# First norm of a diffusion layer: the last token range's column sums, diagonals and spread placed between the middle range's apply steps

## The chip, the cores and the metric

The kernel runs on one core of a Trainium2 chip. The metric is the device time of one execution in microseconds. A run of a kernel is a program of five engines that work side by side and wait for each other by semaphores: PE (matmuls), DVE and ACT (elementwise work, DVE with two tensors), POOL (elementwise work on data outside the matmul accumulators), and SP, which issues DMAs.

## The reference

One layer of a diffusion transformer on 1024 tokens of 1024 channels. After the token mixers, the part that matters here is the first layer norm and the first product of the feed-forward part:

```python
x = _layer_norm(DEEPNORM_ALPHA * x + gate1 * y, ln1_g[l], ln1_b[l])

h = x * (1.0 + scale2) + shift2
y = _conv_ffn(h, w_up[l], conv_w[l], conv_b[l], w_down[l])
...
def _layer_norm(x, g, b):
    mu = jnp.mean(xf, axis=-1, keepdims=True)
    var = jnp.mean(jnp.square(xf - mu), axis=-1, keepdims=True)
    return ((xf - mu) * lax.rsqrt(var + LN_EPS) * g + b).astype(x.dtype)
...
def _conv_ffn(h, w_up, conv_w, conv_b, w_down):
    u = h @ w_up
    ...  # u: convolution over 3 neighbouring tokens, one filter per channel, plus conv_b
    gate, val = jnp.split(u, 2, axis=-1)
    return (jax.nn.silu(gate) * val) @ w_down
```

## The kernel before

Data lie with channels on the 128 partitions: a tensor of 1024 channels is eight blocks f = 0 to 7 (or k, where it is summed over), each with the tokens along its row. Products in float32 are made of three matmuls with split operands (`mm3`, L90 to L92): each operand is a high part and a low part, so `B3` stands for a pair, its high part written by ACT and its low part (value minus high part) by DVE or POOL.

The first norm works on three token ranges, `LN1_S`: 0 to 511, 512 to 767 (the middle range here) and 768 to 1023 (the last range). A token's mean is a sum over partitions, so it is taken by matmuls. `ln_steps` returns a list of eleven steps for a range:

- `stats`: matmuls with a column of ones sum `zs` (the values) and `zq` (their squares) over the channels, L1157 and L1158, into the tile `sta`; then small DVE steps make mean and variance (`mva`, `m2a`, `rsa`, L1159 to L1162), POOL takes the power -1/2 (L1164), and DVE multiplies (`mra`, L1165).
- `diags`: DVE writes two diagonal matrices, `dgra` and `dgma` (L1105).
- `cast`, called the spread here: matmuls with a matrix of ones spread the diagonals over all partitions, into `bca` (L1174); ACT copies the mean's half to `mba` (L1177).
- eight apply steps, in the order f = 0, 4, 1, 5, 2, 6, 3, 7: DVE multiplies (L1182), DVE (f even, L1184) or POOL (f odd, L1186) subtracts, then `emit1` stores the block to DRAM, lets ACT write the high part of `B` and a copy `v` (L1202), and lets DVE or POOL write the low part (L1208).

Each step has a delay beside it. The steps lie in a list, `pend`. Every `mm3` on PE calls `tick` with its columns over 0.8, and `tick` runs the first step of the list as soon as its delay has passed; `drain(n)` runs all but the last n at once. So the list sets where PE's norm matmuls stand between its product matmuls. PE's order is the order of the code; the order of DVE, ACT, POOL and SP is set by a scheduler when the program is built, from the same code, and a step that comes elsewhere in the code can reorder rows of other work there.

After the mixers' last product (`y`), PE makes the up product. Its tiles are `u0_0`, `u1_0`, `u0_1`, `u1_1`, `u0_2`, `u1_2`, each 128 channels by 1024 tokens in the matmul accumulators (`big`, three buffers). The first three tiles are made for the first range, then for the middle range, then for the last range, so that the norm of a range has the products of the range before it as cover. From `u1_1` on a tile is made for all tokens at once. A fourth tile gets the buffer of the first, once its convolution has read it: ACT's L1364 and two DVE steps, L1365 and L1367, into `c0_0`.

```python
def big(name):
    return ps3.tile([P, T], F32, tag="big", name=name, bufs=3)
```

`build(k)`, for k = 0 to 3, forms sums of operand blocks for later products: `t13_k` and `t24_k`, each a first half and a second half, on DVE and POOL; then ACT casts to `T13h_k` and `T24h_k`, and DVE writes the low parts `T13l_k` and `T24l_k` (all L1208). Those steps are put into `pend` after the three ranges, and are first used when the tiles after `u1_2` are made, from 978.8 us on.

## Time and profile before

| | |
|---|---|
| median of 3 runs | 1578.71 us (1578.34 to 1579.38) |
| profiled execution | 1578.46 us, span 1576.7 us |
| PE busy | 1538.4 us, 98% of the span |
| DVE, ACT, POOL busy | 76%, 52%, 47% |
| sums of the last range on PE | from 915.04 us |
| spread of the last range on PE | from 920.76 us |
| first apply of the last range on DVE | 922.23 us |
| `u1_1` begins on PE | 946.12 us |

Rows of a timeline give the start in us from the span's start, the duration, the engine, the line, the operation, the tile written and the tiles read (buffer numbers left out), the shapes, and in brackets how long the engine stood idle before and what released it. Groups of equal rows are merged with a count. A row of a table of stretches gives the stretch, its length, the busy time of PE, PE's weight loads, DVE, ACT and POOL, then PE's granted clock (1.00 is full), the share of the DMA engines and GB/s.

### The profile page before, as it was taken

What the parts mean: (1) busy time and instruction counts of PE and PEld (TensorE: products, weight loads), DVE (VectorE), ACT (ScalarE), POOL (GpSimd) and SP (SyncE); (2) the same over time, 40 slices, a digit from 0 to 9 for tenths busy, and PEclk for the clock granted to TensorE, in tenths of its full rate; (3) what the DMA queues carried; (4) which work ended last, traced back from release to release, by engine and by line L of the source; (5) the groups of instructions that cost most, each with busy time, mean ns of one, the idle gap of its engine ahead of it and who ended that gap; (6) DMA issues with size and microseconds to landing.
All of it is one profiled execution on the core that took longest, in us unless ns stands there. A gap on an engine that the chain in (4) does not pass through costs nothing.

```text
span 1576.7 us, 22297 instructions
## 1 busy us (share of the span) xinstructions
PE 1538.4 (98%) x7804; PEld 1283.1 (81%) x7804; DVE 1199.0 (76%) x1768; ACT 813.8 (52%) x1450; POOL 740.2 (47%) x728
## 2 busy tenths in 40 slices
PE   9999999999999999989999999999999999999997
PEld 7888888888877787777688988888888888888887
DVE  6677976548888677788674788788888887657884
ACT  5323123368887667688430564444444444435552
POOL 0355423526666556555342454566667774021121
PEclk9999999999999999999999999999999999999998
DMA  9776662322247555440550222323334446996821
GB/s 372 270 234 234 224 232 90 110 79 59 63 127 158 130 134 132 115 87 18 179 174 27 92 69 96 118 96 117 109 108 118 110 113 186 367 266 210 258 101 54
DMA packets 112528, 230.00 MB, mean 146 GB/s; under 512 B 12992, under 2 KB 27840, under 8 KB 112320
## 3 DMA queue, kind: packets, MB, share of 16 engines
q1 hardware_dynamic: 97184, 199.72, 38.1%
q0 software_dynamic: 10400, 20.19, 8.4%
q10 hardware_dynamic: 4832, 8.68, 1.5%
q8 instruction: 61, 1.00, 0.3%
q14 instruction: 51, 0.42, 0.1%
HBM read 177.35 MB, written 65.86 MB: 154 GB/s over the span
## 4 chain that ended last, share of the span: by engine, by line
PE 87%; DVE 5%; ACT 3%; issue 2%; POOL 1%; DMA 0%; SPq 0%; DVEq 0%; ACTq 0%; POOLq 0%
PE ptr L611 5%; PE p L90 4%; PE p L91 4%; PE p L92 4%; PE g L90 4%; PE g L92 4%; PE g L91 4%; PE b L92 3%; PE b L91 3%; PE b L90 3%; PE av L632 2%; PE s L494 2%; PE av L633 2%; PE d L92 2%; PE c L92 2%; PE a L92 2%
## 5 line engine op out<-in xcount | busy, mean ns | idle before, releaser
L621 DVE TENSOR_TENSOR ptl<-ptr,pth 128x512 fp32r<-128x512 f32 x188 | 124.5, 684 | 28.0 <-ACT pth L620 26.0
L611 PE MATMUL ptr<-ident,p 128*128 128x128 f32 x816 | 126.8, 278 | 10.5 <-DVE ptl L621 8.2
L620 ACT CAST pth<-ptr 128x512 fp32r<-128x512 f32 x188 | 106.6, 588 | 57.8 <-PE ptr L611 34.2
L87 DVE TENSOR_TENSOR ld<-rd,hd 128x1024 fp32r<-128x1024 f32 x77 | 95.0, 1249 | 49.2 <-ACT hd L82 45.4
L506 ACT ACTIVATE p<-p,nm 128x1024 f32<-128x1024 f32 (+2 forms) x128 | 125.3, 981 | 10.7 <-DVE p L539 10.0
L611 PEld LDWEIGHTS ptr<-ident,p 128*128 128x128 f32 x816 | 93.6, 140 | 40.9 <-DVE ptl L621 13.9
L82 ACT CAST hd<-rd 128x1024 fp32r<-128x1024 f32 x77 | 79.4, 1049 | 82.2 <-PE p L92 58.4
L632 PE MATMUL av<-pth,VT 128*128 128x512 f32 x236 | 104.5, 443 | 0.7 <-ACT avs L638 0.5
L90 PE MATMUL p<-hd 128*128 128x512 f32 x264 | 103.2, 391 | 0.0
L87 POOL TENSOR_TENSOR wlg<-wg,whg 128x512 fp32r<-128x512 f32 x32 | 45.7, 1438 | 122.4 <-ACT whg L82 122.4
L92 PE MATMUL p<-hd,ld 128*128 128x512 f32 x264 | 102.7, 389 | 0.0
L91 PE MATMUL p<-ld,hd 128*128 128x512 f32 x264 | 102.7, 389 | 0.0
L90 PE MATMUL g<-hh,whg 128*128 128x512 f32 x256 | 99.9, 390 | 0.0
L92 PE MATMUL g<-hh,wlg 128*128 128x512 f32 x256 | 99.7, 389 | 0.0
L91 PE MATMUL g<-hl,whg 128*128 128x512 f32 x256 | 99.6, 389 | 0.0
L633 PE MATMUL av<-ptl,VT 128*128 128x512 f32 x236 | 97.7, 414 | 2.0 <-POOL ptl L87 1.8
L539 DVE TENSOR_SCALAR_CACHE_REDUCE p<-s,cvt,nmc 128x1024 f32<-128x1024 f32 x64 | 84.4, 1339 | 12.1 <-PE s L495 11.8
L494 PE MATMUL s<-KL,q 128*128 128x512 f32 (+2 forms) x192 | 76.0, 396 | 2.7 <-ACT p_x L506 2.0
L783 ACT ACTIVATE sg<-g,bgc 128x512 f32<-128x512 f32 x32 | 22.0, 687 | 97.0 <-PE g L92 92.0
L84 POOL TENSOR_SCALAR pth<-prw 128x512 fp32r<-128x512 f32 x48 | 31.0, 646 | 87.2 <-ACT prw L617 62.2
L495 PE MATMUL s<-KL,q 128*128 128x512 f32 (+2 forms) x192 | 71.7, 373 | 0.0
L82 ACT CAST wA<-ru 128x512 fp32r<-128x512 f32 x57 | 35.5, 623 | 67.8 <-PE d L92 36.2
(433 smaller groups left out, 5015.2 us busy)
## 6 DMA issues: line engine op xcount, KB each, us to landing
wml<-in_wmodT_dram SPq DMA_DIRECT2D x48, 512.0 KB
ru<-in_w_up_dram SPq DMA_DIRECT2D x38, 512.0 KB
rd<-td SPq DMA_DIRECT2D x55, 256.0 KB
rd<-sd SPq DMA_DIRECT2D x44, 256.0 KB
rd<-in_w_dn_dram SPq DMA_DIRECT2D x33, 256.0 KB
wm<-in_wmodT_dram SPq DMA_DIRECT2D x16, 512.0 KB
wg<-in_w_g_dram SPq DMA_DIRECT2D x32, 256.0 KB
sgd<-sg ACTq DMA_DIRECT2D x32, 256.0 KB
```

The lines of the kernel that those rows point to most:

```text
L82: nc.scalar.copy(hi, src)
L87: lo_eng.tensor_tensor(out=lo, in0=src, in1=hi.bitcast(F32), op=ALU.subtract)
L90: nc.tensor.matmul(ps, a[0], b[0], start=start, stop=False, skip_group_check=resumed)
L91: nc.tensor.matmul(ps, a[0], b[1], start=False, stop=False, skip_group_check=resumed)
L92: nc.tensor.matmul(ps, a[1], b[0], start=False, stop=stop, skip_group_check=resumed)
L494: nc.tensor.matmul(o, self.q[0][:, hs], ks, start=True, stop=False)
L506: nc.scalar.activation(p, s, AF.Exp, bias=nm[:, h:h + 1], scale=scale, accum_out=sm[:, h:h + 1])
L611: nc.tensor.transpose(tr[:, h * P:(h + 1) * P], self.pslice(h, n), ident)
L620: nc.scalar.copy(hi, tr)
L621: nc.vector.tensor_tensor(out=lo, in0=tr, in1=hi.bitcast(F32), op=ALU.subtract)
L632: nc.tensor.matmul(self.av, v, hi, start=first, stop=False)
L633: nc.tensor.matmul(self.av, v, lo, start=False, stop=self.left == 0)
```

## The change

The last range's steps are no longer put behind the middle range's. When the list gets them it still holds nine steps of the middle range: its spread and its eight applies. The new code puts the sums of the last range behind the fourth apply, its diagonals behind the seventh, its spread behind the eighth, and its applies behind that, with new delays for the three. The numbers of steps that `drain` leaves in the list follow from this.

```diff
-            if f == 6:
+            if f == 6 and si == 1:
                 pend += ln1(si)
+            elif f == 6:
+                (_, st), (_, dg), (_, ca), *ap = ln1(si)
+                n = len(pend) - 4
+                pend[:] = pend[:n] + [(300.0, st)] + pend[n:-1] + [(300.0, dg), pend[-1], (1800.0, ca)] + ap
...
-        drain((len(LN1_S) - 1 - si) * (KT + 3))
+        drain((2 * KT + 6, KT + 1, 0)[si])
```

The diff adds four lines, so line numbers behind it are 4 higher in the new kernel: the old L1367 is its L1371.

On PE, at the up product over the first range (the number behind a tile's name tells which range, k or tile it is, `B7_0` is block 7 for tokens 0 to 511, and the last number is only the buffer's), the piece of the difference at the old place of the sums and the new place of the spread is this:

```order
 L92 MATMUL u1_0_9880<-B6_0_9598,lwu1_0_9728 128x512
-L1157 MATMUL sta2_9997<-onec_70,zs1_9084 128x1
-L1158 MATMUL sta2_9997<-onec_70,zq1_9085 128x1
-L1157 MATMUL sta2_9997<-onec_70,zs1_9084 128x1
-L1158 MATMUL sta2_9997<-onec_70,zq1_9085 128x1
 L90 MATMUL u1_0_9880<-B7_0_9672,hwu1_0_9727 128x512
 L91 MATMUL u1_0_9880<-B7_0_9672,hwu1_0_9727 128x512
 L92 MATMUL u1_0_9880<-B7_0_9672,lwu1_0_9728 128x512
+L1174 MATMUL bca2_10014<-dgra2_9991,onesf_71 128x256
+L1174 MATMUL bca2_10014<-dgma2_9993,onesf_71 128x256
 L90 MATMUL u0_1_9881<-B0_0_9465,hwu0_1_9869 128x512
```

The sums now stand seven k steps further up, ahead of the first matmul of `u1_0`; the spread came six k steps up, from behind k = 5 of `u0_1`.

On DVE, at the end of the middle range's applies (`z` is the value, `bca1` the middle range's spread), the rows before are these:

```order
L1184 TENSOR_TENSOR z2_1_9097<-z2_1_9097,bca1_9891 128x256
L1208 TENSOR_TENSOR B1_1_9922<-v1_9923,B1_1_9922 128x256
L1182 TENSOR_TENSOR z3_1_9109<-z3_1_9109,bca1_9891 128x256
L1208 TENSOR_TENSOR B5_1_9933<-v1_9923,B5_1_9933 128x256
L1182 TENSOR_TENSOR z3_1_9109<-z3_1_9109,bca1_9891 128x256
L1159 TENSOR_SCALAR mva2_9993<-sta2_9997 128x4
L1161 TENSOR_TENSOR m2a2_9994<-mva2_9993 128x2
L1162 SCALAR_TENSOR_TENSOR rsa2_9995<-mva2_9993,m2a2_9994 128x2
L1208 TENSOR_TENSOR B3_1_9967<-v3_9968,B3_1_9967 128x256
L1165 TENSOR_TENSOR mra2_9996<-mva2_9993,rsa2_9995 128x2
L1105 TENSOR_TENSOR dgra2_10019<-ident_58,rsa2_9995 128x256
L1105 TENSOR_TENSOR dgma2_10021<-ident_58,mra2_9996 128x256
```

And from the small step `rsa` on, now:

```order
L1162 SCALAR_TENSOR_TENSOR rsa2_9944<-mva2_9942,m2a2_9943 128x2
L1184 TENSOR_TENSOR z2_1_9097<-z2_1_9097,bca1_9891 128x256
L1208 TENSOR_TENSOR B1_1_9922<-v1_9923,B1_1_9922 128x256
L1165 TENSOR_TENSOR mra2_9945<-mva2_9942,rsa2_9944 128x2
L1182 TENSOR_TENSOR z3_1_9109<-z3_1_9109,bca1_9891 128x256
L1208 TENSOR_TENSOR B5_1_9933<-v1_9923,B5_1_9933 128x256
L1105 TENSOR_TENSOR dgra2_9991<-ident_58,rsa2_9944 128x256
L1105 TENSOR_TENSOR dgma2_9993<-ident_58,mra2_9945 128x256
L1182 TENSOR_TENSOR z3_1_9109<-z3_1_9109,bca1_9891 128x256
L1208 TENSOR_TENSOR B3_1_9982<-v3_9983,B3_1_9982 128x256
```

All six small steps of the last range now stand ahead of the middle range's last L1182. On POOL the power, L1164, likewise moved ahead of the subtracts of f = 3 and 7.

On DVE, where the first convolution is reached (`c0_0` reads the accumulator of `u0_0`, and `t13_2`, `t24_2` and so on are the sums of `build`), the rows before are these:

```order
L1208 TENSOR_TENSOR T13l_1_10373<-t13_1_10342,T13h_1_10372 128x1024
L1208 TENSOR_TENSOR t13_2_10412<-v2_9947,z2_0_9094 128x512
L1365 SCALAR_TENSOR_TENSOR c0_0_10235<-u0_0_9879,cvt_69,c0_0_10235 128x1023
L1208 TENSOR_TENSOR t24_2_10427<-v2_9947,t13_2_10412 128x512
L1367 SCALAR_TENSOR_TENSOR c0_0_10235<-u0_0_9879,cvt_69,c0_0_10235 128x1023
```

And now:

```order
L1208 TENSOR_TENSOR T13l_1_10373<-t13_1_10342,T13h_1_10372 128x1024
L1208 TENSOR_TENSOR t13_2_10412<-v2_9962,z2_0_9094 128x512
L1208 TENSOR_TENSOR t24_2_10427<-v2_9962,t13_2_10412 128x512
L1208 TENSOR_TENSOR t13_3_10478<-v3_9983,z3_0_9106 128x512
L1208 TENSOR_TENSOR t24_2_10427<-z2_0_9094,t24_2_10427 128x512
L1208 TENSOR_TENSOR T13l_2_10443<-t13_2_10412,T13h_2_10442 128x1024
L1208 TENSOR_TENSOR T24l_2_10456<-t24_2_10427,T24h_2_10455 128x1024
L1369 SCALAR_TENSOR_TENSOR c0_0_10235<-u0_0_9879,cvt_69,c0_0_10235 128x1023
L1208 TENSOR_TENSOR t24_3_10481<-v3_9983,t13_3_10478 128x512
L1371 SCALAR_TENSOR_TENSOR c0_0_10235<-u0_0_9879,cvt_69,c0_0_10235 128x1023
```

`t13_3`, the second `t24_2`, `T13l_2`, `T24l_2` and `t24_3` moved ahead of the second step of `c0_0`. On ACT, `T13h_2` and `T24h_2` moved ahead of `c0_0`'s first step. The order of SP is the same, and so is that of every engine from the tiles behind `u1_2` on.

## The prediction

> **What bounds the kernel now.** I read the page first, then PE's waits over the whole run, then the busy time by stretches, then the timelines of PE, DVE, POOL and ACT from 905 to 950 us, where the change acts.

> ```profile
> span 1576.7 us, 22297 instructions
> PE 1538.4 (98%) x7804; PEld 1283.1 (81%) x7804; DVE 1199.0 (76%) x1768; ACT 813.8 (52%) x1450; POOL 740.2 (47%) x728
> PE u L91 <- DVE B L1208: 2.9, 1, 2.9
> 932.85:935.90 3.05, 0.17 (x3) 0.01 (x1) 3.05 (x4) 3.05 (x5) 3.05 (x3) 0.89 0.13 43
> 935.90:942.10 6.20, 6.20 (x29) 6.20 (x30) 6.20 (x5) 4.66 (x5) 3.54 (x3) 0.50 0.00 0
> 946.10:978.80 32.70, 32.70 (x147) 27.07 (x146) 29.74 (x27) 13.75 (x17) 12.15 (x8) 1.00 0.33 113
> 978.80:1540.00 561.20, 561.20 (x2548) 467.19 (x2547) 450.39 (x429) 274.46 (x362) 269.97 (x164) 1.00 0.53 160
> ```

> PE is busy for 98% of the span, so a gain must come out of its gaps. The third line is its only long wait near the change (one, of 2.9 us, the longest single one of the run): the up product over the last token range wants the low half of `B3`, which DVE has not written. The stretches (length, then busy time of PE, PEld, DVE, ACT and POOL, then PE's granted clock) show that it costs twice: PE stands for 3 us, and for the next 6.2 us works at clock 0.50. From 946.1 to 1540 PE has no gap, so whatever PE's arrival at 946.1 gains or loses is carried to the end whole.

> The wait's exact price, from PE's timeline:

> ```profile
> 923.02 0.28 PE L90 MATMUL u<-B,hwu 128*128 128x256 f32 x1
> ...
> 932.73 0.28 PE L90 MATMUL u<-B,hwu 128*128 128x256 f32 x1
> 935.90 0.58 PE L91 MATMUL u<-B,hwu 128*128 128x256 f32 x1 [2.88 <-DVE B L1208]
> 936.28 0.42 PE L92 MATMUL u<-B,lwu 128*128 128x256 f32 x1
> ...
> 942.04 0.29 PE L92 MATMUL u<-B,lwu 128*128 128x256 f32 x1
> ...
> 946.12 0.40 PE L90 MATMUL u<-B,hwu 128*128 128x512 f32 x1
> ```

> The 81 matmuls from 923.02 to 932.73 come every 0.120 us, the 27 from 936.28 to 942.04 every 0.213. At full pace the one at 935.90 would have started at 932.85 (3.05 lost), and the 28 up to 942.04 lost 6.14 - 28 x 0.120 = 2.78. So 5.83 us are to be had, 0.37%, and PE would begin `u1_1` (the row at 946.12) at 940.29.

> **The change, part by part.** Nothing is added or removed: the same four sum matmuls, seven small DVE and POOL steps, two spread matmuls and one copy stand elsewhere. None of them issues a DMA, and SP's queue has the same order. First, how much earlier the last range's applies (L1182 on) start:

> ```profile
> 910.28 0.39 PE L90 MATMUL u<-B,hwu 128*128 128x512 f32 x1
> ...
> 914.82 0.39 PE L92 MATMUL u<-B,lwu 128*128 128x512 f32 x1
> 915.04 0.28 PE L1157 MATMUL sta<-onec,zs 128*128 128x1 f32 x2
> ...
> 920.76 0.59 PE L1174 MATMUL bca<-dgra,onesf 128*128 128x256 f32 x2
> 912.64 0.51 DVE L1208 TENSOR_TENSOR B<-v,B 128x256 fp32r<-128x256 f32 x1 [0.78 <-ACT v L1202]
> 913.63 0.96 DVE L1208 TENSOR_TENSOR B<-v,B 128x256 fp32r<-128x256 f32 x1
> 914.51 0.41 DVE L1182 TENSOR_TENSOR z<-z,bca 128x256 f32<-128x256 f32 x1
> 916.03 0.16 DVE L1159 TENSOR_SCALAR mva<-sta 128x4 f32<-128x4 f32 x1 [1.11 <-PE sta L1158]
> 918.47 0.42 DVE L1105 TENSOR_TENSOR dgma<-ident,mra 128x256 f32<-128x256 f32 x1
> 915.00 0.73 POOL L1186 TENSOR_TENSOR z<-z,mba 128x256 f32<-128x256 f32 x1 [0.69 <-DVE z L1182]
> 917.21 0.82 POOL L1164 TENSOR_TENSOR rsa<-rsa,mhalf 128x2 f32<-128x2 f32 x1
> 921.83 0.37 ACT L1177 COPY mba<-bca 128x256 f32<-128x256 f32 x1 [4.29 <-PE bca L1174]
> 922.23 0.42 DVE L1182 TENSOR_TENSOR z<-z,bca 128x256 f32<-128x256 f32 x1 [3.01 <-ACT mba L1177]
> ```

> - The sums move seven k steps up PE, from 915.04 to 910.28, 4.76 earlier. Their cost on PE stays (they are in the stream either way).
> - The spread moves six k steps up: a step is 3 x 0.227 (the 20 matmuls from 910.28 to 914.82), so 920.76 - 6 x 0.681 = 916.7 at the earliest. The applies can come 4.1 earlier at most.
> - DVE pays. Its four small steps and two diagonals now stand ahead of the middle range's last apply (914.51) instead of behind: 4 x 0.16 + 2 x 0.34 = 1.3, plus a wait for POOL's power (0.82) and a short one of the first small step for the sums, with the middle range's subtract behind it; the 0.78 that DVE idled at 912.64 takes up about that much. Best, the last apply starts at 915.8; then POOL's subtract (0.73) and two ACT casts (1.1) follow, ACT copies the mean (0.37), and the first apply of the last range starts at about 918.5: 3.7 earlier than 922.23. Worst, POOL's operations alternate with the diagonals, as one already stretches `B` to 0.96 at 913.63: 917.3, and some 920.3: 1.9 earlier. I take 2.4, near the worst, since every DVE row here that met a POOL operation was stretched. PE may wait up to 0.8 us for the diagonals; that is swallowed by the wait below.

> Second, what DVE does after those applies:

> ```profile
> 934.89 2.37 DVE L1208 TENSOR_TENSOR B<-v,B 128x256 fp32r<-128x256 f32 x2
> 937.19 1.21 DVE L1208 TENSOR_TENSOR T13l<-t,T13h 128x1024 fp32r<-128x1024 f32 x1
> 938.32 1.21 DVE L1208 TENSOR_TENSOR T24l<-t,T24h 128x1024 fp32r<-128x1024 f32 x1
> 939.46 2.30 DVE L1208 TENSOR_TENSOR T13l<-t,T13h 128x1024 fp32r<-128x1024 f32 x1
> 941.68 0.68 DVE L1208 TENSOR_TENSOR t<-v,z 128x512 f32<-128x512 f32 x1
> 942.28 1.27 DVE L1365 SCALAR_TENSOR_TENSOR c<-u,cvt,c 128x1023 f32<-128x1023 f32 x1
> 943.48 0.67 DVE L1208 TENSOR_TENSOR t<-v,t 128x512 f32<-128x512 f32 x1
> 944.07 1.27 DVE L1367 SCALAR_TENSOR_TENSOR c<-u,cvt,c 128x1023 f32<-128x1023 f32 x1
> 938.48 2.20 POOL L1208 TENSOR_TENSOR t<-v 128x512 f32<-128x512 f32 x1 [1.50 <-DVE T13l L1208]
> 941.84 1.68 POOL L1208 TENSOR_TENSOR t<-v 128x512 f32<-128x512 f32 x1 [1.16 <-DVE T13l L1208]
> ```

> Up to the second `T13l` the order is the old one, so with the applies 2.4 earlier `B3` is written at about 933.5 instead of 935.85; PE wants it at 932.85, and its wait shrinks to 0.6 us. The old wait is as good as gone.

> But `u1_1` needs one of the three `big` buffers, and the one it gets is that of `u0_0`, free when the convolution has read it: the second step, L1367, at 944.07 + 1.27 = 945.34. PE came at 946.12, with 0.78 to spare, and only because it had lost 5.83 us before. The new order puts five more DVE steps ahead of that L1367: `t13_3`, the second `t24_2`, `T13l_2`, `T24l_2` and `t24_3`. A `t` costs 0.60 (941.68 to 942.28), a `T` 1.13 (937.19 to 938.32): 3 x 0.60 + 2 x 1.13 = 4.1. That is the floor. At 939.46 `T13l` took 2.30 beside a POOL row of 2.20: they took turns. The POOL row at 941.84 cost DVE nothing, because DVE was in the convolution; in the new order it meets `t24_2`, which would wait until 943.52 instead of starting at 942.3, 1.2 more, so 5.3 at the top. ACT puts `T13h_2` and `T24h_2` ahead of its own convolution step too, and that is just ready when DVE is. I take 5.2.

> [...]

> So L1367 ends at 945.34 + 5.2 - 2.4 = 948.1, and PE, which is there by about 941, waits some 7 us. `u1_1` starts at 948.2 instead of 946.12: +2.1.

> Then the clock. After a 3 us wait it was 0.50 until 942.04, so after 7 us I expect the same. A 512-wide matmul goes from 0.227 to 0.427 (twice 0.213), so 47% of the spell is lost: 2.9 for the 6.14 us seen. The mean clock of 0.89 in the wait puts the fall 0.22 x 3.05 = 0.67 before its end, so the whole spell was 6.8 us, nearly all of it after the restart; that is the long end, 3.2. How the spell falls on the restart is chance, so the short end is half of what was seen, 1.4. I take 2.4.

> [...]

> **Sum:** -0.7 (the spare time, with 0.05 for the semaphore) + 5.2 - 2.4 + 2.4 = +4.5 us. After `u1_1` the next buffers (L1367 of `c1_0`, three DVE rows or some 3.5 us later) are needed 11 us on, so nothing else waits, and PE's gapless stretch carries the 4.5 to the end. The profiled execution took 1578.46 us (span 1576.7), 0.25 under the median of 1578.71: 1578.5 + 4.5 = 1583.0. Lowest: -0.7 + 4.1 - 3.7 + 1.4 = +1.1, 1579.6. Highest: -0.7 + 5.3 - 1.9 + 3.2 = +5.9, 1584.4; with half a microsecond for the scatter of the runs 1584.9.

> **Rivals.**
> 1. Faster: PE's wait goes and `u1_1` finds its buffer free. That needs L1367 done by 940.3, 5 us before its old end, with 4.1 us more ahead of it: the applies would have to start 9 us earlier, and the spread allows 4.1. It would give 1578.5 - 5.8 = 1572.6. For it speaks only that the one named wait is truly shortened. 4%, with anything else that gains.
> 2. A draw: the same trade, but DVE gets its early start (3.7) and little blocking, or the clock spell is short: +1.1 to +3.1, about 1580.7. For it: the terms at their good ends. Against: all of them must be good at once. 20%.
> 3. The change does not do what it says: POOL's turns hold up the diagonals so much that the last range starts no earlier. Then the five steps still stand in front: -0.7 + 5.2 + 2.4 = +6.9, 1585.4. Against: the sums leave PE 4.8 us earlier whatever DVE does. 6%.

> **Chances.** A measurement of this kernel tells about 0.2%, 3.2 us, from no change. The forecast (+3.2 to +5.9) has 70%; with rival 3 slower has 76%; the draw 20%; faster 4%. The range 1579.6 to 1584.9 holds the draw and the forecast, and leaves out the faster rival and most of the third.

> **What the profile of after would show.** Right: sums at about 910.3 and spread at 916.7 to 917.5; PE's wait for `B3` under 1.5 us or gone; a new PE wait of 5 to 9 us at L90 `u` for DVE `c` L1371 (the old L1367), starting near 941; clock 0.50 for 3 to 7 us after it; and `u1_1` starting at 947 to 949. Wrong: no such wait, or `u1_1` before 946. The forecast fails if DVE's `T` steps of k = 2 run unblocked while the applies start at 918.5, or if the clock comes back within 2 us of the restart.

## The result, and the profile after

The changed kernel took 1583.03 us (median of 10 runs, 1581.14 to 1583.97) where the kernel before, on the same chip, took 1578.93 us (10 runs, 1576.19 to 1580.16). The ratio is 1.0030, with a 95% interval of 1.0021 to 1.0038: slower by 4.1 us, as forecast (1583.0, range 1579.6 to 1584.9). Three far slower runs are left out of the medians below: 1901.59 and 1702.34 us in experiment 4, at a mean granted clock of 0.75 and 0.85, and 3094.25 us in experiment 3, at full clock.

The page of the profiled execution (1583.14 us), span and busy time:

```profile
span 1581.3 us, 22301 instructions
PE 1539.0 (97%) x7804; PEld 1283.0 (81%) x7804; DVE 1197.2 (76%) x1768; ACT 814.2 (51%) x1450; POOL 738.3 (47%) x728
```

PE does the same work in a span that is 4.6 us longer. Its waits (engine, line and tile, what it waited for, total, count, longest):

```profile
PE u L90 <- DVE c L1371: 7.2, 1, 7.2
```

The wait of 2.9 us for `B3` is gone from the list, and this one, now the longest single one of the run, has come: `u1_1` wants the buffer that `c0_0`'s second DVE step (L1371, the old L1367) has still to read. PE's timeline:

```profile
907.33 0.59 PE L1174 MATMUL bca<-dgra,onesf 128*128 128x256 f32 x2
...
911.64 0.28 PE L1157 MATMUL sta<-onec,zs 128*128 128x1 f32 x2
...
918.04 0.59 PE L1174 MATMUL bca<-dgra,onesf 128*128 128x256 f32 x2
...
934.23 0.35 PE L91 MATMUL u<-B,hwu 128*128 128x256 f32 x1
...
949.05 0.77 PE L90 MATMUL u<-B,hwu 128*128 128x512 f32 x1 [7.18 <-DVE c L1371]
949.62 0.63 PE L91 MATMUL u<-B,hwu 128*128 128x512 f32 x1
...
952.59 0.40 PE L92 MATMUL u<-B,lwu 128*128 128x512 f32 x1
```

The first row is the spread of the middle range, which the change doesn't touch. In the kernel before it stands at

```profile
905.97 0.59 PE L1174 MATMUL bca<-dgra,onesf 128*128 128x256 f32 x2
```

so this execution was already 1.36 us late before anything differs, and its times are compared after taking off 1.36. Then the sums stand at 910.28 and the last range's spread at 916.68; the prediction had 910.3 and 916.7. At 934.23 the product over `B3` goes on without a gap. The first eight matmuls of `u1_1` come every 0.44 us on average, from 952.59 on every 0.23. DVE in the same stretch (start, duration):

```profile
915.81 0.96 DVE L1105 TENSOR_TENSOR dgra<-ident,rsa 128x256 f32<-128x256 f32 x1
...
917.57 0.41 DVE L1182 TENSOR_TENSOR z<-z,bca 128x256 f32<-128x256 f32 x1
...
920.47 0.42 DVE L1182 TENSOR_TENSOR z<-z,bca 128x256 f32<-128x256 f32 x1
...
937.76 2.31 DVE L1208 TENSOR_TENSOR T13l<-t,T13h 128x1024 fp32r<-128x1024 f32 x1
940.00 0.68 DVE L1208 TENSOR_TENSOR t<-v,z 128x512 f32<-128x512 f32 x1
940.71 1.67 DVE L1208 TENSOR_TENSOR t<-v,t 128x512 f32<-128x512 f32 x1
942.30 0.68 DVE L1208 TENSOR_TENSOR t<-v,z 128x512 f32<-128x512 f32 x1
942.90 0.68 DVE L1208 TENSOR_TENSOR t<-z,t 128x512 f32<-128x512 f32 x1
943.51 1.21 DVE L1208 TENSOR_TENSOR T13l<-t,T13h 128x1024 fp32r<-128x1024 f32 x1
944.70 1.23 DVE L1208 TENSOR_TENSOR T24l<-t,T24h 128x1024 fp32r<-128x1024 f32 x1
945.84 1.28 DVE L1369 SCALAR_TENSOR_TENSOR c<-u,cvt,c 128x1023 f32<-128x1023 f32 x1
947.03 0.68 DVE L1208 TENSOR_TENSOR t<-v,t 128x512 f32<-128x512 f32 x1
947.63 1.28 DVE L1371 SCALAR_TENSOR_TENSOR c<-u,cvt,c 128x1023 f32<-128x1023 f32 x1
```

The rows at 940.00 and 940.71 are `t13_2` and the first half of `t24_2`, which stood ahead of `c0_0`'s second step before, too. Then come the five that did not: `t13_3`, the second half of `t24_2`, `T13l_2`, `T24l_2` and, between `c0_0`'s two steps, `t24_3`. DVE is never idle here; it does the wrong work first. The 1.67 at 940.71 stands beside POOL's half of `t13_3`, in POOL's timeline:

```profile
940.15 1.68 POOL L1208 TENSOR_TENSOR t<-v 128x512 f32<-128x512 f32 x1 [1.16 <-DVE T13l L1208]
```

ACT's step of `c0_0`, behind `T13h_2` and `T24h_2`, ends at 945.77, just before DVE takes it up at 945.84:

```profile
944.57 1.20 ACT L1368 ACTIVATE c<-u,cvt 128x1024 f32<-128x1024 f32 x1
```

So DVE's five steps and ACT's two casts ran level. Experiments 1 and 2 below move both together; no run parts them.

### The profile page after: what moved, and what is told of

Read it like the earlier page. It is cut to its first block, busy times and chain, and to the rows that moved or that the text cites. A ratio compares the mean times of both kernels' runs of the same rounds, so it can differ in the third digit from the quotient of the medians.

```text
span 1581.3 us, 22301 instructions
## 1 busy us (share of the span) xinstructions
PE 1539.0 (97%) x7804; PEld 1283.0 (81%) x7804; DVE 1197.2 (76%) x1768; ACT 814.2 (51%) x1450; POOL 738.3 (47%) x728
## 4 chain that ended last, share of the span: by engine, by line
PE 86%; DVE 6%; ACT 3%; issue 2%; POOL 1%; DMA 1%; SPq 0%; DVEq 0%; ACTq 0%; POOLq 0%
PE ptr L611 5%; PE p L90 4%; PE p L92 4%; PE p L91 4%; PE g L90 4%; PE g L92 4%; PE g L91 4%; PE b L92 3%; PE b L91 3%; PE b L90 3%; PE av L632 2%; PE s L494 2%; PE d L91 2%; PE c L91 2%; PE a L91 2%; PE av L633 2%
## 5 line engine op out<-in xcount | busy, mean ns | idle before, releaser
L506 ACT ACTIVATE p<-p,nm 128x1024 f32<-128x1024 f32 (+2 forms) x128 | 125.4, 982 | 10.8 <-DVE p L539 10.1
L90 PE MATMUL p<-hd 128*128 128x512 f32 x264 | 103.2, 391 | 0.0
L92 PE MATMUL p<-hd,ld 128*128 128x512 f32 x264 | 102.8, 389 | 0.0
L91 PE MATMUL p<-ld,hd 128*128 128x512 f32 x264 | 102.7, 389 | 0.0
L90 PE MATMUL g<-hh,whg 128*128 128x512 f32 x256 | 99.9, 390 | 0.0
L92 PE MATMUL g<-hh,wlg 128*128 128x512 f32 x256 | 99.7, 389 | 0.0
L91 PE MATMUL g<-hl,whg 128*128 128x512 f32 x256 | 99.6, 389 | 0.0
```

The lines of the kernel that those rows point to most:

```text
L90: nc.tensor.matmul(ps, a[0], b[0], start=start, stop=False, skip_group_check=resumed)
L91: nc.tensor.matmul(ps, a[0], b[1], start=False, stop=False, skip_group_check=resumed)
L92: nc.tensor.matmul(ps, a[1], b[0], start=False, stop=stop, skip_group_check=resumed)
L506: nc.scalar.activation(p, s, AF.Exp, bias=nm[:, h:h + 1], scale=scale, accum_out=sm[:, h:h + 1])
```

## The experiments

Theory: all of the loss is `u1_1`'s wait for `u0_0`'s buffer, because DVE now runs five `T` steps (steps of `build`, `t` and `T` alike) ahead of the end of `c0_0`'s convolution, with the half clock behind that wait; the early norm itself gains. Rivals: the small norm steps among the middle range's applies cost; the half clock alone costs; the slip that was there before the change's place. One table for all, with times counted from the middle range's spread, so that what happened earlier in a run drops out (row 4 has its trace from the second run of experiment 4 and its median from the first):

| kernel | spread of the middle range | `u1_1` starts, from there | lost at half pace in `u1_1` | end of the span, from there | median us |
|---|---|---|---|---|---|
| before | 905.97 | 40.15 | 0 | 670.73 | 1578.6 to 1579.0 |
| changed | 907.33 | 41.72 | 1.72 | 673.97 | 1583.03 |
| 1, convolution first | 904.82 | 35.39 | 0 | 665.98 | 1574.42 |
| 1b, and ahead of k = 1 | 907.28 | 34.34 | 0 | 665.12 | 1574.17 |
| 2, before with the five steps ahead | 907.42 | 44.99 | 2.07 | 677.58 | 1585.58 |
| 3, sums alone | 908.36 | 40.13 | 0 | 670.64 | 1579.43 |
| 4, before, convolution first | 907.40 | 38.46 | 0 | 669.10 | 1578.92 |
| 5, changed, more delay | 907.62 | 45.86 | 2.87 | 679.28 | 1587.33 |
| 6, changed, no turn | 906.37 | 40.73 | 2.34 | 673.73 | 1582.11 |

In each row the fifth column less that of the kernel before equals the third and fourth together, less those of before, within 0.2 us (changed: 1.57 + 1.72 = 3.29 against 3.24; 2: 4.84 + 2.07 = 6.91 against 6.85; 1: -4.76 against -4.75). So `u1_1`'s start and the half pace in it account for every difference between these traces. The kernel before had 1578.63 (22 runs) beside 1 to 4, 1579.01 (15 runs) beside the others.

**1. The change, with the convolution first.** The build steps of k = 2 and 3 are queued on DVE and ACT behind `c0_0`'s instructions (an edge of order alone, no wait; `ia` is `c0_0`'s ACT step, `iv` its second DVE step):

```diff
+        if c == 0:
+            first.extend((ia.ins, iv.ins))
...
+    def behind(fn):
+        def run():
+            with tc.issue_after(first[0]), tc.issue_after(first[1]):
+                fn()
+        return run
...
-        pend += [(BLD, fn) for fn in build(k)]
+        pend += [(BLD, behind(fn) if k > 1 else fn) for fn in build(k)]
```

> The changed kernel, with the T steps of k = 2 and 3 queued on DVE and ACT behind c0_0's convolution; the early norm of the last range stays. Theory (the loss is u1_1 waiting for u0_0's buffer, because DVE runs five T steps ahead of c0_0's second step): DVE reaches that step right behind T13l_1, two steps of 1.2 after 940.0, so it ends at 942.4 instead of 948.9; PE, there at 941.9, waits some 0.6 us instead of 7.2 and keeps its full clock. 6.5 us come back, and up to 1.7 of half clock: 1583.0 - 6.5 - 1.7 is 1574.8 at best; if the T steps that now come later hold up the products of j = 3 (DVE has about 3 us of idle time up to there, and 5 us more to do), up to 1578. So 1574.8 to 1578, and no PE wait over 1.5 us at L90. Rival A (the small norm steps and the diagonals between the middle range's applies, and POOL's turns there, are what costs): nothing changes up to 935, and the time stays near 1583. Rival B (the half clock alone costs, whatever waits): about 1581.

Measured: 1574.42 us, ratio to the kernel before 0.9972 (0.9960 to 0.9983). Its PE waits, then PE's and DVE's timelines:

```profile
PE u L90 <- DVE c L1371: 0.9, 1, 0.9
```

```profile
940.21 0.47 PE L90 MATMUL u<-B,hwu 128*128 128x512 f32 x1 [0.85 <-DVE c L1371]
```

```profile
935.24 2.31 DVE L1208 TENSOR_TENSOR T13l<-t,T13h 128x1024 fp32r<-128x1024 f32 x1
937.47 1.27 DVE L1369 SCALAR_TENSOR_TENSOR c<-u,cvt,c 128x1023 f32<-128x1023 f32 x1
938.78 1.28 DVE L1371 SCALAR_TENSOR_TENSOR c<-u,cvt,c 128x1023 f32<-128x1023 f32 x1
```

With the steps out of the way, the convolution follows `T13l` at once; the wait of 7.2 becomes 0.9, PE keeps its clock (1.00 from 935.9 to 942.0), and the kernel is 4.2 us (0.28%) faster than the kernel before. That is 0.4 below the expected range, whose best case was 1574.8. Rival A (the small steps cost, 1583) falls: they stand here as in the changed kernel. So does rival B (the half clock alone costs, 1581): of the 7.99 us that this trace gains on the changed kernel's, 6.33 are `u1_1`'s start. The later `T` steps held up nothing that shows in the table.

**2. The kernel before, with the five steps ahead.** The reverse: the norm stays, and `c0_0`'s steps are queued behind the `T` steps that precede them in the changed kernel.

```diff
+            queue(first[to], [i.name for i in new if i.engine == mybir.EngineType.DVE])
+            if to == 1:
+                queue(first[0], [i.name for i in new if i.engine == mybir.EngineType.Activation])
...
+    AHEAD = {(2, 2): 1, (2, 3): 1, (3, 0): 1, (3, 1): 2}
     for k in range(4):
-        pend += [(BLD, fn) for fn in build(k)]
+        pend += [(BLD, ahead(fn, AHEAD[k, n]) if (k, n) in AHEAD else fn) for n, fn in enumerate(build(k))]
```

(`AHEAD` names the step of `build`, and whether `c0_0`'s first or second DVE step goes behind it. Edges of the same kind keep the weights of `u0_2` and `u1_2` on DVE and the later convolutions behind `c0_0`, as in the changed kernel. On DVE `t24_3` and `T24l_2` stand in exchanged places; on ACT the casts of those weights and `c1_0`'s step come ahead of `c0_0`'s.)

> The kernel before (the norm of the last range where it was), with DVE's T steps put ahead of c0_0's convolution exactly as the changed kernel has them (T13h_2 and T24h_2 ahead of it on ACT). Theory: c0_0's second step ends 5.3 us later than in the kernel before, at 950.6 instead of 945.3; PE, there at 946.1 after the old wait for B3, waits a second time, 4.5 us, and loses another 1.4 to 3.2 to the half clock: 1578.9 + 4.5 + 1.4 to 3.2 = 1584.8 to 1586.6. So slower than the changed kernel, since the early norm's gain of 3.1 us is missing. Rival A (the small norm steps cost, not the order of the T steps): 1579.

Measured: 1585.58 us, ratio 1.0044 (1.0031 to 1.0056). PE's waits, and PE's timeline at both of them:

```profile
PE u L90 <- DVE c L1374: 7.4, 1, 7.4
PE u L91 <- DVE B L1208: 2.9, 1, 2.9
```

```profile
937.35 0.39 PE L91 MATMUL u<-B,hwu 128*128 128x256 f32 x1 [2.88 <-DVE B L1208]
937.57 0.28 PE L92 MATMUL u<-B,lwu 128*128 128x256 f32 x1
...
952.41 0.77 PE L90 MATMUL u<-B,hwu 128*128 128x512 f32 x1 [7.37 <-DVE c L1374]
```

The order of the `T` steps alone makes the kernel 7.0 us slower, more than the whole change does. One thing came out otherwise than expected. After the wait for `B3`, the same 2.88 us as before, PE went on at full pace (0.22 from the first row to the next, then 0.12). So it came to `u1_1` some 2.7 us earlier than expected and waited 7.4 instead of 4.5. The time, 1585.58, still lies in the range expected, since `c0_0`'s second step decided it, not PE's arrival.

**3. The sums alone.** Sums where the change puts them; diagonals and spread behind the middle range's last apply.

```diff
-                pend[:] = pend[:n] + [(300.0, st)] + pend[n:-1] + [(300.0, dg), pend[-1], (1800.0, ca)] + ap
+                pend[:] = pend[:n] + [(300.0, st)] + pend[n:] + [(4500.0, dg), (2000.0, ca)] + ap
-        drain((2 * KT + 6, KT + 1, 0)[si])
+        drain((2 * KT + 6, KT + 2, 0)[si])
```

> The change in part: the sums of the last range stand where the change puts them, its diagonals and its spread stay behind the middle range's last apply as before; DVE does the four small steps between the middle range's applies, and its later order is the old one. Theory: the spread leaves PE when it did, so the last range's applies, the B3 wait and c0_0's convolution stay where they were: 1578.9, between 1578 and 1580. Rival A (the small steps among the applies are what costs): 1 to 4 us slower, 1580 to 1583.

Measured: 1579.43 us, ratio 1.0003 (0.9994 to 1.0012). The last range's spread and `u1_1`'s first matmul on PE:

```profile
923.15 0.59 PE L1174 MATMUL bca<-dgra,onesf 128*128 128x256 f32 x2
...
948.49 0.40 PE L90 MATMUL u<-B,hwu 128*128 128x512 f32 x1
```

The spread stands 14.79 after the middle range's, as before, and `u1_1` starts 40.13 after it, against 40.15. The four small steps among the applies cost nothing that reaches PE; the earlier sums alone win nothing, so it is the place of the diagonals and the spread that sets when the last range starts.

**4. The kernel before, convolution first.** The edit of experiment 1 without the change.

> The kernel before, with the same queueing of the T steps of k = 2 and 3 behind c0_0's convolution and nothing of the change. Theory: u1_1 found its buffer free in the kernel before, so an earlier convolution alone buys nothing; the wait of 2.9 us for B3 and the half clock behind it stay: 1578.9, between 1578 and 1580. Then any gain of the kernel with the change and the queueing over the kernel before is the early norm's own. Rival (the order of the convolution is worth time by itself): 1574 to 1577 here too.

> The kernel before with the T steps of k = 2 and 3 behind c0_0's convolution once more, for its trace. Theory: PE waits 2.9 us for B3 as before and begins u1_1 within 0.3 us of the kernel before, counted from the spread of the middle range, though c0_0's second step ends some 1.2 us earlier.

Measured: 1578.92 us, ratio 0.9999 (0.9990 to 1.0009); the single execution of the second run 1578.26. So the earlier convolution alone buys nothing in the median, and the 4.2 us of experiment 1 need the early norm with it. Its PE waits and PE's timeline:

```profile
PE u L91 <- DVE B L1208: 2.9, 1, 2.9
PE u L90 <- DVE c L1367: 0.9, 1, 0.9
```

```profile
937.32 0.39 PE L91 MATMUL u<-B,hwu 128*128 128x256 f32 x1 [2.87 <-DVE B L1208]
937.54 0.28 PE L92 MATMUL u<-B,lwu 128*128 128x256 f32 x1
...
945.86 0.47 PE L90 MATMUL u<-B,hwu 128*128 128x512 f32 x1 [0.86 <-DVE c L1367]
```

The expectation of the trace was wrong: `u1_1` began 1.7 us earlier than in the kernel before, because here too no half clock followed the wait for `B3` (0.22 us from the first row to the next, then 0.12), and PE then stood 0.86 us at `c0_0`'s buffer. So the half clock behind that wait came in some profiled executions (the kernel before, 3) and not in others (2, 4), and in the kernel before it was mostly hidden: without it PE would have met `c0_0`'s second step at 945.34, 0.7 us before the 946.12 at which it came.

**1b. The steps of k = 1 behind the convolution too** (`k > 0` for `k > 1`).

> As the kernel with the change and the T steps of k = 2 and 3 behind c0_0's convolution, with those of k = 1 behind it too. There PE still waited 0.85 us for c0_0's second step (1.13 us lost between two matmuls, 939.08 to 940.21), because T13l_1 took 2.31 us in front of it. Theory: the second step now ends about 2 us before PE comes, the wait goes, and 1.0 us more is gained: 1574.4 - 1.0 = 1573.4, unless the later T steps of k = 1 hold up the products of j = 3 (then 1574 to 1577). Rival (the remaining wait is not DVE's order but u0_0's own end): the 0.85 us stays and the time is 1574.4.

Measured: 1574.17 us, ratio 0.9970 (0.9958 to 0.9981). The wait is gone:

```profile
938.13 1.28 DVE L1369 SCALAR_TENSOR_TENSOR c<-u,cvt,c 128x1023 f32<-128x1023 f32 x1 [2.64 <-ACT c L1368]
939.45 1.28 DVE L1371 SCALAR_TENSOR_TENSOR c<-u,cvt,c 128x1023 f32<-128x1023 f32 x1
```

```profile
941.62 0.40 PE L90 MATMUL u<-B,hwu 128*128 128x512 f32 x1
```

`u1_1` starts 34.34 after the middle range's spread instead of 35.39: the 1.0 us is there in the trace, but the medians (1574.17, 1574.42) don't tell the two kernels apart. The margin is 0.9 us, not 2, since DVE now waits for ACT's step. Both versions beat the kernel before and the changed one.

**5. The changed kernel with a longer wait.**

```diff
+        for _ in range(3 if c == 0 else 0):
+            nc.vector.tensor_scalar(out=t, in0=t, scalar1=1.0, scalar2=0.0, op0=ALU.mult, op1=ALU.add)
```

(The loop stands between `c0_0`'s two DVE steps. An edge of order keeps the later convolutions behind `c0_0`.)

> The changed kernel with three more DVE steps (c0_0 times one plus nothing, in place) between the two steps of c0_0's convolution, some 0.8 us each (an estimate from 0.48 us for 512 elements and 0.18 for 64); T13l_3 slips in behind them (1.2). Theory (PE's start of u1_1 follows c0_0's second step one for one, and the half clock behind a long wait costs the same whatever the wait's length): the wait grows from 7.2 to some 10.8 us, the time by 3.6 to 1586.6; at half pace again 6 to 12 matmuls, 1.4 to 3.2 us lost. Rival A (the lost clock grows with the wait): 2.6 us lost instead of 1.7, 1587.5. Rival B (PE has other work to give, or the wait is not on the way to the end): 1583.

Measured: 1587.33 us, ratio 1.0054 (1.0041 to 1.0067).

```profile
947.91 3.09 DVE L1372 TENSOR_SCALAR c<-c 128x1024 f32<-128x1024 f32 x3
```

```profile
953.48 0.76 PE L90 MATMUL u<-B,hwu 128*128 128x512 f32 x1 [11.33 <-DVE c L1373]
...
959.53 0.40 PE L92 MATMUL u<-B,lwu 128*128 128x512 f32 x1
```

The rows took 1.03 us each, not 0.8, and with `T13l` the wait grew by 4.15 us, `u1_1`'s start by 4.14: one for one, so rival B falls. At half pace 14 matmuls came, 6.05 - 14 x 0.227 = 2.87 lost, between the theory's bounds (1.4 to 3.2) but also near rival A's 2.6. The median rose by 4.30 over the changed kernel's, hardly more than the wait, but it is not known sharply enough to part the theory from rival A; experiment 6 adds a shorter wait.

**6. The changed kernel without POOL's turn.** POOL's half of `t13_3` waits for `c0_0`'s second step (`add_manual_dep` from it to `first[1]`, with a semaphore); DVE's order is the changed kernel's, row for row.

> The changed kernel with DVE's order kept, in which POOL's half of t13_3 starts only behind c0_0's second step, so that it no longer runs beside the second t24_2 on DVE. Theory (the two take turns: beside POOL's 1.68 the DVE step took 1.67, alone it takes 0.68): t24_2 takes 0.68, c0_0's second step ends 1.0 earlier and the wait falls from 7.2 to 6.2; the time is 1583.0 - 1.0 = 1582.0, give or take 1 for the phase of the half clock. Rival (t24_2 was long for another reason, such as its own wait for a buffer): it stays at 1.67 and the wait at 7.2.

Measured: 1582.11 us, ratio 1.0022 (1.0012 to 1.0032). The wait, the row of `t24_2` on DVE, and `u1_1`'s rows on PE:

```profile
PE u L90 <- DVE c L1377: 6.2, 1, 6.2
```

```profile
939.74 0.69 DVE L1208 TENSOR_TENSOR t<-v,t 128x512 f32<-128x512 f32 x1
```

```profile
947.10 0.77 PE L90 MATMUL u<-B,hwu 128*128 128x512 f32 x1 [6.21 <-DVE c L1377]
...
951.94 0.44 PE L92 MATMUL u<-B,lwu 128*128 128x512 f32 x1
```

The step (`t24_2`'s first half; the expectation calls it the second) takes 0.69 us instead of 1.67, and the wait is 1.0 shorter: the turn with POOL's 1.68 made 1.0 of the wait, where the prediction counted 1.2. The trace shows it; the medians (1582.11 and 1583.03) are too near each other to. And after a shorter wait (6.2) more was lost at half pace (11 matmuls, 4.84 - 11 x 0.227 = 2.34) than after the changed kernel's 7.2 (1.72). So the wait's length alone does not set the lost clock, though the longest of the four waits did lose the most.

## Why the prediction was right, point by point

- *Where PE's norm matmuls go.* Sums and spread stand where forecast, to 0.1 us. The wait for `B3` is gone; 0.6 us of it were to stay.
- *How much earlier the last range's applies start.* Forecast 2.4, bounds 1.9 to 3.7. The row at 920.47, less 1.36, is 919.11 against 922.23: 3.1. The middle range's last apply came at 917.57, aligned 916.2; best was put at 915.8, worst at 917.3. Both diagonals did take 0.96 beside POOL instead of 0.42, and still the last apply came only 0.4 after its best case: the value was chosen too near the worst end. Its reason, "every DVE row here that met a POOL operation was stretched", does not hold in the kernel before: the small step at 916.03, which reads the accumulators (`sta`), took its usual 0.16 inside POOL's two rows:

```profile
915.68 1.44 POOL L1208 TENSOR_TENSOR B<-v,B 128x256 fp32r<-128x256 f32 x2
```

  This term was mis-sized by 0.7.
- *Five DVE steps ahead of the convolution.* Forecast 5.2, bounds 4.1 to 5.3. `c0_0`'s second step ended at 948.91, aligned 947.55; before, 945.34, which would be 942.22 with applies 3.12 earlier. So the steps cost 5.33, the upper bound. Experiment 6 shows the blocked `t24_2` (1.0) in it, experiment 2 the term without the early norm: there `u1_1` starts 4.84 later than in the kernel before, 5.5 with the spare time.
- *The spare time.* -0.7, the end of `c0_0`'s second step against PE's arrival. Right in this trace, but only because PE had been slowed by the half clock; experiment 4 shows that without it the spare time is gone. Buffer and clock were two limits within 0.7 us of each other: of the 5.83 us that "are to be had", 0.7 were, as long as the convolution came no earlier. That is why rival 1 needed `c0_0` done by 940.3.
- *The half clock after the new wait.* Forecast 2.4, bounds 1.4 to 3.2; measured 1.72 in this trace. In the four kernels with a long wait it was 1.72, 2.07, 2.34 and 2.87, mean 2.25. So the forecast fits the mean, and the changed kernel's trace was a low draw.
- *The sum.* -0.7 + 5.33 - 3.12 = +1.5 (`u1_1` came 1.57 later; forecast +2.1), and 1.72 make +3.3 where +4.5 was forecast. That the median hit 1583.0 to a tenth is luck: both misses lie on the slow side, the forecast started from 1578.5 (the profiled execution) where the median before is 1578.93, the medians differ by 4.1 with an interval of 3.3 to 6.0, and the place where the change begins alone came between 904.8 and 908.4 in the nine profiles.
- *The rivals.* Faster (1572.6): its condition, that `c0_0` be done when PE comes, did not hold in the change as made; once it nearly holds (1) or holds (1b), the time is 1574.4 and 1574.2. The draw: by the trace it was close, +3.3 against its upper end of 3.1; two of the three terms came out on their good side. No effect on the applies: excluded, they started 3.1 earlier.

## What to carry to other kernels

When an edit moves work ahead of a wait, list what stands ahead of the *next* wait in the new order, not only whether the old wait shrinks: here 3.1 us were gained on the operands and 5.3 lost because DVE's freed time was given to steps first needed 30 us later. Work that frees an accumulator buffer for the next product belongs ahead of work whose result is needed later; edges of order alone turned 4.1 us of loss into 4.2 of gain. And count times from a row that the edit cannot reach before two single profiles are subtracted.

## What the runs showed of the hardware that was not expected

```profile
941.90:949.00 7.10, 0.00 (x0) 0.00 (x0) 7.10 (x9) 5.38 (x6) 1.14 (x1) 0.77 0.00 0
```

```profile
942.00:953.40 11.40, 0.15 (x2) 0.00 (x0) 11.33 (x13) 9.57 (x11) 1.69 (x2) 0.67 0.00 0
```

  A mean of 0.77 over 7.10 us is 2 x 0.23 x 7.10 = 3.3 us at 0.50, so the clock fell at 945.7; in 5 it fell at 945.9 (2 x 0.33 x 11.40 = 7.5 before 953.4). An estimate worked out so, from the mean clocks and up to the first row at full pace, puts the spell at some 6.8 us in the kernel before (935.24 to 942.04), 6.9 in the changed one (945.7 to 952.59), 6.8 in experiment 6 (945.2 to 951.94), 6.9 in 2 (949.85 to 956.75), 6.8 in 3 (937.6 to 944.42), and 13.6 in 5 (945.9 to 959.5). What is lost after the restart is some half of what is then left of the spell (1.72 of 3.54 us in the changed kernel, 2.07 of 4.34 in 2, 2.34 of 4.84 in 6, 2.87 of 6.05 in 5), not a share of the wait.
- The same wait of 2.87 to 2.88 us cost the clock in the kernel before and in experiment 3, and left it whole in 2 and 4 (1.00 from 934.3 to 937.3 in both). By the same estimate the clock fell 2.2 us after PE's last matmul in the kernel before (933.0 to 935.24) and in 3 (935.4 to 937.6). The longer waits (6.2 to 11.3 us) all lost the clock, 3.7 to 4.8 us after PE's last matmul. What parts the two cases of the same wait is not shown: no run moves that wait. But the prediction counted the 2.78 us at half clock as a fixed part of that wait's price, and in 2 and 4 the wait came without it.
- An in-place DVE multiply and add over 128 x 1024 took 1.03 us (3.09 for three in experiment 5), near the 1.21 of a step with two inputs (`T13l` at 943.51 in the changed kernel).
